# Seven products over six of eight k-tiles: a decoder layer on one core of a Trainium2 chip, with its buffers cut to make room

## The chip, the core and the metric

The kernel is one program on one core of a Trainium2 chip. The time is device microseconds (us) from start to end of one execution. Five engines run beside each other, each through its own instruction stream in order, and wait for one another by semaphores: PE (matrix products), DVE (vector), ACT (activation and copies), POOL and SP (here it only issues DMAs). PEld is PE's loading of stationary operands, which overlaps PE's products.

## What is computed

One layer with two token mixers over 2048 prompt tokens and 8 sample tokens, all in fp32:

```
xn   = rms_norm(x) * g_pre                      # 1024 columns
proj = xn @ w_in                                # 1024 x 11280, split into qkv_a z_a a_a b_a qkv_b z_b gate_a gate_b
a    = gated delta rule, 8 heads, over silu(short conv(qkv_a)), gated with silu(z_a), @ w_proj_a
b    = dilated window attention, 3 groups of 4 heads, combined by softmax weights, gated with silu(z_b), @ w_proj_b
y    = x + rms_norm((sigmoid(gate_a) * a + sigmoid(gate_b) * b) @ w_out) * g_post
```

The outputs also hold the states and caches of both mixers.

## The kernel before

**Precision.** A product in fp32 is made of three passes over operands split into a high and a low part: hi*hi, hi*lo, lo*hi. Three matmuls of one 128 x 128 block of W against one row of X stand together; the text calls them a triple (`three`, L991).

**In-projection.** The prompt is worked through in two halves of 1024 tokens, each again in two blocks of 512 (`th`). Columns of w_in come as tiles of 128, two tiles per step (`step`, L983). Of the eight k-tiles of 128 rows, the first KS = 4 go through a Winograd scheme: a 2 x 2 block product (token blocks by k halves, k halves by the two column tiles) in seven products instead of eight, each over KH = KS/2 k-tiles; the other 8 - KS are multiplied plainly (`rest`). A step is thus 7*KH + 4*(8 - KS) triples, 30 with KS = 4. In the first half a step is run twice (256 and 260 columns, the 4 extra being sample tokens), in the second once with 512 columns. There are 44 steps per half; the very first of all is a plain one (`opening`, L927). Sums of X (`sums`, L733) and of W (`wsplit`, L796) feed the seven products. X lies split and transposed in SBUF rows XS (seven sums by KH) and XP (plain k-tiles); `transpose` (L688) makes four PE transposes per row and `xevac` (L554) splits it. For the second half the rows are written anew as the last step of the first half lets go of each.

**W.** SP loads each pair of W tiles into two buffers (`raws`). `wsplit` forms sums and writes six split pieces (`evs` 0 to 5) into six slots of 512 columns; `done` in `step` gives a slot back after its last product. A step uses, in this order, products 1 (slot 0), 7 (slot 1), 6 (slot 2), 2 (slot 0), rest (3), 5 (2), 4 (slot 4), rest (3), 3 (slot 1), rest (slot 5); the last rest runs after the first product of the next step.

**The other work.** Each finished tile is copied out by `sink` (L855) into a page, one of 17 SBUF buffers of 1040 columns. `gdn` (L1212) is one delta-rule head: short conv of its k, q and v tiles (`conv`, L1174), decay tables, an inverse by 31 small steps on a lane buffer (`inverse`, L1359), and a loop over 8 chunks through the state `st`. `attn` (L1479) is one head of one group, `combine` joins three. `sample_gdn` and `sample_attn` work on the sample tokens during the second half. `final` (L1740) makes the last three products for four token groups.

**What sets the order.** A planner at build time (`Scheduler`, L87) runs all these as coroutines with costs and priorities and writes each engine's stream. A string, `ORDER` (L2171), sets in which order column tiles are projected: G is a head's k, q, v tiles, Z its gate tile, a one attention group (every fourth a is the z tile), g an output gate, x and y the claims for the second half's X, S, T, C those of the sample work and the conv state. In that same order page claims (`claim`, `admitter`) are granted, first come first served, out of as many tokens as there are pages: a claim that does not fit holds back all claims behind it, and `sink` holds its PSUM bank until its tile's claim is granted. A head claims 1 + 1 + 4 + 1 pages and 1 for its gate tile; `gdn` gives one back after its q part and one after its v part. `claim_page(keep)` in `final` takes a page only while more than `keep` are free.

Of the kernel before, what the change touches and what calls it, by code (L numbers as in the profile page):

```python
# [26 lines left out]
KS = 4  # L27
# [426 lines left out]
def build(nc, tc, ctx, I, O):  # L454
# [18 lines left out]
    NPAGE = 17  # L473
# [3 lines left out]
    wslots = Pool([(tl(f"wh{i}", [128, 512], F32R), tl(f"wl{i}", [128, 512], F32R)) for i in range(6)])  # L477
    tbuf = tl("wt", [128, 2 * KH, 128])
# [8 lines left out]
    szg = tl("szg", [128, 12, NB])  # L487
# [79 lines left out]
    def xsamples(pg):  # L567

        page = yield Acquire(pages, 1)
        fxs = page[:, :96].rearrange("p (k t c) -> p k t c", t=2, c=4)  # L570
# [27 lines left out]
    def prep(hf, b, admit):  # L598
# [11 lines left out]
        def scales():  # L610
            st["s2"] = yield Acquire(pages, 1)
            g = I["g_pre"]
            yield K.load(st["s2"][:, :w], bass.AP(tensor=g.tensor, offset=g.offset, ap=[[0, 128], [1, w]]))
# [74 lines left out]
    def transpose(hf, st, keys, summed=None):  # L688
        pg, m = st["pg"], 128 * KH
        for key in keys:  # L690
# [7 lines left out]
            else:  # L698
                n, k = key
                o = 128 * k + m * (n in (2, 3, 4))  # L700
                if n == 6:
                    src = [st["s2"][:, m * i + o:m * i + o + 128] for i in range(4)]
                else:
                    src = [pg[4 * (n in (4, 5)) + i][:, o:o + 128] for i in range(4)]
# [28 lines left out]
    def sums(st, ev):  # L733
        m = 128 * KH
        for i in range(4):
            p, q, s2 = st["pg"][i], st["pg"][4 + i], st["s2"][:, m * i:m * i + m]
# [6 lines left out]
    def transposed1(hf, st, toks):  # L743
# [10 lines left out]
        pages.release(*(pg[i] for i in range(4, 8)), st["s2"])  # L754
        tok.release(*toks, st["toks"][4])
# [3 lines left out]
        if hf == 0:  # L759
            yield Wait(xs_ev[1])  # L760
            pages.release(pg[8])
            tok.release(*st["toks"][5:])
# [25 lines left out]
    def wput(src, ev):  # L788

        hi, lo = slot = yield Acquire(wslots, 1)  # L790
        n = src.shape[1]
        yield K.copy(hi[:, :n], src)
        yield K.tt(lo[:, :n], src, hi[:, :n].bitcast(F32), OP.subtract)
        ev.set(slot)

    def wsplit():  # L796
        for at, (kind, us, evs) in enumerate(jobs):
# [4 lines left out]
            if kind == "ab":  # L802
# [3 lines left out]
                slot = yield Acquire(wslots, 1)  # L806
# [5 lines left out]
            elif kind == "plain":  # L812
                m = 128 * KH
                for j in range(2):
                    yield from wput(f[j][:, :2 * m], evs[j])
                    yield from wput(f[j][:, 2 * m:], evs[2 + j])
                T = tbuf.rearrange("p a b -> p (a b)")
                for j in range(2):
                    yield K.tt(T[:, m * j:m * j + m], f[j][:, m:2 * m], f[j][:, :m], OP.subtract)
                yield from wput(T[:, :2 * m], evs[4])  # L820
            elif kind == "pair":
# [3 lines left out]
                T = tbuf.rearrange("p a b -> p (a b)")  # L825
                t1, t2 = (T[:, m * j:m * j + m] for j in range(2))
                yield from wput(f[0][:, :2 * m], evs[0])
                yield K.tt(t1, b12, b11, OP.subtract)
                yield K.tt(b12, b22, b12, OP.subtract)
                yield from wput(f[1][:, :2 * m], evs[1])  # L830
                yield K.tt(t2, b22, t1, OP.subtract)
                yield from wput(T[:, :2 * m], evs[2])
                yield from wput(r1, evs[3])
                yield K.tt(b21, b21, t2, OP.subtract)
                yield from wput(b21, evs[4])
                yield from wput(r2, evs[5])
            else:
                if at < len(jobs) - 2:
                    for j in range(2):
                        yield from wput(f[0][:, 512 * j:512 * j + 512], evs[1 + j])  # L840
# [14 lines left out]
    def sink(t, th, gi, c0, n, bank, pool):  # L855
# [43 lines left out]
        if t.left == 0:  # L899
# [4 lines left out]
            elif k == "z" and t.half == 0:  # L904
                yield K.pcopy(szg[:, t.idx, :], pg[:, HT:HT + NB])
# [21 lines left out]
    def opening(work):  # L927
# [3 lines left out]
        for th in range(2):  # L931
# [17 lines left out]
            if th == 1:  # L949
                wslots.release(*(e.val for e in evs[:5]))  # L950
            for gi, (c0, w) in enumerate(gemm_groups(0)):
                yield from ab_tile(0, tab, evab, th, gi, c0, w, mainb[2 * gi])
        wslots.release(evab[0].val)

    def ab_tile(hf, t, evs, th, gi, c0, w, pool):
# [12 lines left out]
    def inproj(hf, work):  # L968
# [3 lines left out]
        for at, (kind, tiles, evs) in enumerate(work):  # L972
            slots = {}
            for gi, (c0, w) in enumerate(gemm_groups(hf)):
                if kind == "ab":
                    for th in range(2):
                        yield from ab_tile(hf, tiles[0], evs, th, gi, c0, w, mainb[2 * th])
                    wslots.release(evs[0].val)
# [4 lines left out]
    def step(hf, tiles, evs, slots, gi, c0, w, end, last):  # L983
# [7 lines left out]
        def three(acc, key, hl, off, first, final):  # L991
            hi, lo = (x[:, off:off + 128] for x in hl)
# [5 lines left out]
        def product(acc, n, slot, off, first=False):  # L998
            hl = yield from wk(slot)
            for k in range(KH):  # L1000
                yield from three(acc, (n, k), hl, off + 128 * k, first and k == 0, k == KH - 1)
                if last:
                    if hf == 0:
                        xfree[n, k].set()
                    else:
# [12 lines left out]
        def done(*ns):  # L1018
            if end:
                wslots.release(*(slots[n] for n in ns))  # L1020
# [66 lines left out]
    seb = tl("seb", [128, 2, GH, NB])  # L1087

    def ab_tables(hf, t, work):
# [62 lines left out]
        if hf == 0:  # L1152
# [9 lines left out]
            yield K.copy(seb.rearrange("p a h b -> p (a h b)"), bank[:, :128])  # L1162
            side.release(bank)
        pages.release(ab, pg, tmp, cmat)
# [47 lines left out]
    def gdn(hf, h, tk, tq, tv, tz, work, done):  # L1212
# [57 lines left out]
        tok.release(toks.pop())  # L1270
# [3 lines left out]
        tok.release(toks.pop())  # L1274
# [41 lines left out]
    def gdn_q(tq, kT, e, row, sm, tb, h, ev):  # L1316
        qT = yield from conv(tq)
        gp = yield Acquire(pages, 1)
        yield K.load(gp[:, :HT], bass.AP(tensor=row.tensor, offset=row.offset, ap=[[0, 128], [1, HT]]))
# [24 lines left out]
        pages.release(gp)  # L1344
# [385 lines left out]
    def wcols(slot, off, n):  # L1730

        o = off % 512
        return [x[:, o:o + n] for x in slot[off // 512]]
# [182 lines left out]
    def sample_gdn(tiles, abdone):  # L1916
# [25 lines left out]
        pg = yield Acquire(pages, 1)  # L1942
        for i in range(2):
# [409 lines left out]
```

## Time and profile before

| | |
|---|---|
| median of 3 runs (lowest to highest) | 3048.79 us (3048.49 to 3049.93) |
| profiled execution: its own time | 3050.04 us |
| profiled execution: span from first to last instruction | 3048.2 us |
| PE, PEld, DVE, ACT, POOL busy share of the span | 99%, 88%, 72%, 40%, 5% |
| mean granted share of PE's clock | 0.996 |
| instructions | 55885 |

PE's busy time counts overlapping matmuls once, so what a matmul costs is read from the distance of one start to the next. "Idle before" is how long an engine stood still ahead of an instruction, with what ended it. PEclk is the granted share of full clock.

### The profile page before, as it was taken

The page shows a single profiled execution, that of the slowest core. Times are in us where ns is not written, and L with a number is a line of the kernel's source. Part 1 is how long each engine was busy: PE and PEld are TensorE (multiplying, and loading weights), DVE is VectorE, ACT ScalarE, POOL GpSimd, SP SyncE. Part 2 cuts the span into 40 slices and gives each one's busy share as a digit, 9 for nine tenths or more (in the row PEclk, how much of TensorE's full clock was granted, in tenths as well). Part 3 has the DMA queues.
Part 4 walks back from the last instruction along what each step waited for, and adds up shares of the span by engine and source line. Part 5 has one row for each costly group of instructions (what it writes and reads, how often), then busy time and mean ns, then how long its engine had stood idle before and what let it go on. Part 6 is the DMA issues. An engine that isn't in the chain of part 4 may idle for free.

```text
span 3048.2 us, 55885 instructions
## 1 busy us (share of the span) xinstructions
PE 3010.0 (99%) x20879; PEld 2692.0 (88%) x20879; DVE 2199.2 (72%) x5978; ACT 1212.9 (40%) x3444; POOL 141.1 (5%) x239
## 2 busy tenths in 40 slices
PE   7999999999999999999999999999999999999999
PEld 7999999999999999978887888888888888897887
DVE  6777767786778686767586868597988486666765
ACT  5545444344435443433442534343434343313121
POOL 1000000000000000000000000000000000000000
PEclk9999999999999999999999999999999999999999
DMA  4323242332233325332244332336452236565463
GB/s 125 94 73 89 58 112 71 99 85 83 70 98 89 89 79 147 110 85 81 73 121 124 88 88 80 105 96 186 137 158 86 76 100 180 176 204 197 149 226 117
DMA packets 468760, 343.46 MB, mean 113 GB/s; under 512 B 88745, under 2 KB 411825, under 8 KB 468480
## 3 DMA queue, kind: packets, MB, share of 16 engines
q1 hardware_dynamic: 468488, 339.89, 38.1%
q8 instruction: 164, 2.69, 0.4%
q14 instruction: 108, 0.88, 0.1%
HBM read 261.40 MB, written 80.97 MB: 112 GB/s over the span
## 4 chain that ended last, share of the span: by engine, by line
PE 94%; DVE 3%; DMA 2%; ACT 1%; issue 0%; SPq 0%; POOL 0%; DVEq 0%; POOLq 0%; ACTq 0%
PE bank L251 89%; PE bank L267 5%; DVE pg L311 1%; DMA wr<-in_w_in 0%; DVE wl L316 0%; DVE pg L316 0%; SPq L400 0%; DMA pg<-in_cache_v_w 0%; DMA pg<-in_x_prompt 0%; DMA pg<-in_state_gdn 0%; DMA pg<-gate 0%; ACT L280 0%; DMA ghh<-in_g_head_norm 0%; DVE wh L355 0%; DVE junk L311 0%
## 5 line engine op out<-in xcount | busy, mean ns | idle before, releaser
L280 ACT ACTIVATE pg<-bank 128x256 f32<-128x256 f32 (+7 forms) x741 | 331.8, 460 | 759.4 <-PE bank L251 690.0
L316 DVE TENSOR_TENSOR wl<-wr,wh 128x512 fp32r<-128x512 f32 x595 | 383.5, 647 | 21.3 <-ACT wh L280 3.3
L355 DVE CAST wh<-wr 128x512 fp32r<-128x512 f32 (+1 forms) x384 | 153.0, 399 | 206.9 <-PE bank L251 184.0
L251 PE MATMUL bank<-xp7s,wh 128*128 128x512 f32 (+3 forms) x1196 | 302.1, 328 | 0.0
L251 PE MATMUL bank<-xp6s,wh 128*128 128x512 f32 (+3 forms) x1132 | 290.1, 330 | 0.0
L251 PE MATMUL bank<-xp5s,wh 128*128 128x256 f32 (+3 forms) x1100 | 276.3, 327 | 0.0
L280 ACT ACTIVATE wh<-wr 128x512 fp32r<-128x512 f32 (+1 forms) x213 | 129.8, 611 | 351.9 <-PE bank L251 292.1
L251 PE MATMUL bank<-xp4s,wh 128*128 128x260 f32 (+2 forms) x1068 | 267.5, 326 | 1.6 <-DVE xp4s L311 1.6
L316 DVE TENSOR_TENSOR bank<-bank,etmp 128x256 f32<-128x256 f32 (+2 forms) x260 | 134.9, 519 | 129.4 <-PE bank L251 126.3
L251 PEld LDWEIGHTS bank<-xp7s,wh 128*128 128x128 f32 x1196 | 198.4, 188 | 17.5 <-issue 1.7
L251 PEld LDWEIGHTS bank<-xp6s,wh 128*128 128x128 f32 (+1 forms) x1132 | 189.2, 188 | 17.2 <-issue 0.8
L251 PEld LDWEIGHTS bank<-xp5s,wh 128*128 128x128 f32 (+1 forms) x1100 | 183.0, 188 | 14.7 <-issue 0.2
L251 PE MATMUL bank<-xp7s,wl 128*128 128x512 f32 (+3 forms) x592 | 195.0, 329 | 0.0
L251 PEld LDWEIGHTS bank<-xp4s,wh 128*128 128x128 f32 x1068 | 176.1, 188 | 14.9 <-DVE xp4s L311 1.8
L280 ACT ACTIVATE prob<-bank 128x512 f32<-128x512 f32 (+4 forms) x224 | 105.2, 482 | 208.7 <-PE bank L251 120.8
L311 DVE SCALAR_TENSOR_TENSOR pg<-pg,convw,pg 128x1024 f32<-128x1024 f32 x144 | 183.9, 1277 | 2.8 <-ACT pg L280 1.3
L251 PE MATMUL bank<-xp6s,wl 128*128 128x512 f32 (+2 forms) x560 | 184.9, 330 | 0.0
L251 PE MATMUL bank<-xp5s,wl 128*128 128x512 f32 (+2 forms) x544 | 178.5, 328 | 0.0
L251 PE MATMUL bank<-xs1k,wh 128*128 128x512 f32 (+4 forms) x708 | 177.8, 334 | 0.0
L251 PE MATMUL bank<-xp4s,wl 128*128 128x256 f32 (+2 forms) x528 | 172.5, 327 | 0.0
L251 PE MATMUL bank<-xs6k,wh 128*128 128x512 f32 (+3 forms) x680 | 171.3, 334 | 0.0
L251 PE MATMUL bank<-xs7k,wh 128*128 128x512 f32 (+3 forms) x680 | 169.9, 333 | 0.0
(302 smaller groups left out, 7474.8 us busy)
## 6 DMA issues: line engine op xcount, KB each, us to landing
wr<-in_w_in SPq DMA_DIRECT2D x176, 512.0 KB
pg<-in_x_prompt SPq DMA_DIRECT2D x32, 512.0 KB
pg<-grow SPq DMA_DIRECT2D x32, 512.0 KB
wr<-in_w_proj_a SPq DMA_DIRECT2D x32, 512.0 KB
wr<-in_w_out SPq DMA_DIRECT2D x32, 512.0 KB
pg<-og SPq DMA_DIRECT2D x24, 520.0 KB
pg<-gate SPq DMA_DIRECT2D x24, 512.0 KB
out<-pg SPq DMA_DIRECT2D x20, 512.0 KB
```

The costliest lines, as they stand in the source:

```text
L251: nc.tensor.matmul(out, lhsT, rhs, start=start, stop=stop, skip_group_check=shared)
L267: nc.tensor.transpose(out, in_, ident[:k, :k])
L280: return ("act", c, lambda: nc.scalar.activation(out, in_, func, **kw))
L311: lambda: nc.vector.scalar_tensor_tensor(out, in0, scalar, in1, op0=op0, op1=op1, **kw))],
L316: return ("dve", self._vcost(out, in0, in1), lambda: nc.vector.tensor_tensor(out, in0, in1, op=op))
L355: alts.append(("dve", self._vcost(out, in_, fast=True), lambda: nc.vector.tensor_copy(out, in_)))
```

## The change

KS goes from 4 to 6: seven products over three k-tiles each and two plain k-tiles. More rows of X are kept (25 instead of 22), and to make room:

- 15 pages instead of 17; a head claims 3 work pages instead of 4 and gives none back early; prep claims rise (7 to 8 and 5 to 6), as the X sums now take two pages.
- The W slots become three kinds: 3 of 768 columns (pieces 0 to 2), 1 of 384 (piece 4 and the small a/b tile), 2 of 256 (pieces 3 and 5). Sums of W are made in place in the raw buffers, and the buffer `wt` goes.
- `conv` works in place in halves of 512 columns through the four `prob` buffers, which attention, inverse and others share.
- `gdn_q` puts the decay row into the one lane buffer that `inverse` also uses, instead of a page.
- Two small tables (`szg`, `seb`) move to DRAM; 12 POOL copies become 12 DMA stores, with one more store and three loads.
- `ORDER` is another string for both halves.
- At the end of the second half three freed X rows become W slots.

```diff
-KS = 4
+KS = 6
-    NPAGE = 17
+    NPAGE = 15
-    wslots = Pool([(tl(f"wh{i}", [128, 512], F32R), tl(f"wl{i}", [128, 512], F32R)) for i in range(6)])
-    tbuf = tl("wt", [128, 2 * KH, 128])
+    wslots, wthird, wrest = Pool([]), Pool([]), Pool([])
+    for i, (pool, w) in enumerate([(wslots, 256 * KH)] * 3 + [(wthird, 128 * KH)] + [(wrest, 128 * (8 - KS))] * 2):
+        pool.free.append((tl(f"wh{i}", [128, w], F32R), tl(f"wl{i}", [128, w], F32R), pool))
...
-    def wput(src, ev):
-        hi, lo = slot = yield Acquire(wslots, 1)
-        n = src.shape[1]
-        yield K.copy(hi[:, :n], src)
-        yield K.tt(lo[:, :n], src, hi[:, :n].bitcast(F32), OP.subtract)
+    def wput(parts, ev, pool=wslots):
+        hi, lo, _ = slot = yield Acquire(pool, 1)
+        c = 0
+        for src in parts:
+            v = slice(c, c := c + src.shape[1])
+            yield K.copy(hi[:, v], src)
+            yield K.tt(lo[:, v], src, hi[:, v].bitcast(F32), OP.subtract)
         ev.set(slot)
...
-                yield from wput(f[0][:, :2 * m], evs[0])
-                yield K.tt(t1, b12, b11, OP.subtract)
+                yield from wput([f[0][:, :2 * m]], evs[0])
+                yield K.tt(b11, b12, b11, OP.subtract)
                 yield K.tt(b12, b22, b12, OP.subtract)
-                yield from wput(f[1][:, :2 * m], evs[1])
-                yield K.tt(t2, b22, t1, OP.subtract)
-                yield from wput(T[:, :2 * m], evs[2])
-                yield from wput(r1, evs[3])
-                yield K.tt(b21, b21, t2, OP.subtract)
-                yield from wput(b21, evs[4])
-                yield from wput(r2, evs[5])
+                yield from wput([f[1][:, :2 * m]], evs[1])
+                yield K.tt(b22, b22, b11, OP.subtract)
+                yield from wput([b11, b22], evs[2])
+                yield from wput([r1], evs[3], wrest)
+                yield K.tt(b21, b21, b22, OP.subtract)
+                yield from wput([b21], evs[4], wthird)
+                yield from wput([r2], evs[5], wrest)
...
     def conv(t):
-        cp = yield Acquire(pages, 1)
-        c, w = cp[:, :HT], convw[:, t.idx]
-        yield K.scaled(c, pg[:, 3:3 + HT], w[:, 3:4])
-        for i in (2, 1, 0):
-            yield K.stt(c, pg[:, i:i + HT], w[:, i:i + 1], c, OP.mult, OP.add)
-        yield K.act(pg[:, :HT], c, AF.Tanh, scale=0.5)
-        yield K.stt(c, pg[:, :HT], 1.0, c, OP.add, OP.mult)
-        pages.release(pg)
-        return cp
+        for o in (0, HT // 2):
+            c = yield Acquire(prob_t, 1)
+            yield K.scaled(c, pg[:, o + 3:o + 3 + HT // 2], w[:, 3:4])
+            for i in (2, 1, 0):
+                yield K.stt(c, pg[:, o + i:o + i + HT // 2], w[:, i:i + 1], c, OP.mult, OP.add)
+            yield K.act(pg[:, o:o + HT // 2], c, AF.Tanh, scale=0.5)
+            yield K.stt(pg[:, o:o + HT // 2], pg[:, o:o + HT // 2], 1.0, c, OP.add, OP.mult)
+            prob_t.release(c)
+        return pg
...
-        tok.release(toks.pop())
         toks = toks + (yield Wait(tv.admit))
...
-        tok.release(toks.pop())
...
     def gdn_q(tq, kT, e, row, sm, tb, h, ev):
         qT = yield from conv(tq)
-        gp = yield Acquire(pages, 1)
+        ln = yield Acquire(lanes, 1)
+        gp = ln[0]
...
-    ORDER = ("GZaaGaZaGaagZGgaZagGZaagGagagZGagaZGaZagggggggxgyg",
-             "gGgZggaagGaZSagGaZaGaZgaggGaagTZGaZaCggGaaZgGZaggag")
+    ORDER = ("GaaGZgaaZGaaZGZagagGZaagGaaZggGaagZGgagZagggggxgyg",
+             "GZgaaggGagSagZgGaaZGaggZaGagagTgZGggaZagGaaGZZaggaC")
...
-            preps = [[claim(7), claim(4)], None]
+            preps = [[claim(8), claim(4)], None]
...
-            work = claim(4)
+            work = claim(3)
```

## Rows read from the trace of the kernel before

**Rows 1.** The page: busy time of each engine; the chain that ended last, by engine.
```profile
PE 3010.0 (99%) x20879; PEld 2692.0 (88%) x20879; DVE 2199.2 (72%) x5978; ACT 1212.9 (40%) x3444; POOL 141.1 (5%) x239
...
PE 94%; DVE 3%; DMA 2%; ACT 1%; issue 0%; SPq 0%; POOL 0%; DVEq 0%; POOLq 0%; ACTq 0%
```

**Rows 2.** Timeline of PE, one step of the first half (start us, duration us).
```profile
1002.83 0.40 PE L251 MATMUL bank<-xs1k,wh 128*128 128x256 f32 x2
...
1013.49 0.40 PE L251 MATMUL bank<-xs1k,wh 128*128 128x260 f32 x2
...
1024.15 0.60 PE L267 MATMUL bank<-cst,pg 128*128 128x128 f32 x4
1024.51 0.36 PE L251 MATMUL bank<-xp7s,wl 128*128 128x260 f32 x1
1024.71 0.40 PE L251 MATMUL bank<-xs1k,wh 128*128 128x256 f32 x2
```

**Rows 3.** Timeline of PE, two triples of the second half.
```profile
1929.70 0.63 PE L251 MATMUL bank<-xs1k,wh 128*128 128x512 f32 x2
...
1930.39 0.62 PE L251 MATMUL bank<-xs1k,wh 128*128 128x512 f32 x2
```

**Rows 4.** Groups of DVE by form: count, busy us, mean ns of one.
```profile
L316 DVE TENSOR_TENSOR wl<-wr,wh 128x512 fp32r<-128x512 f32 x508 | 347.0, 686 | 20.2 <-ACT wh L280 3.3 <-PE bank L251 2.3
L311 DVE SCALAR_TENSOR_TENSOR pg<-pg,convw,pg 128x1024 f32<-128x1024 f32 x144 | 183.9, 1277 | 2.8 <-ACT pg L280 1.3
L355 DVE CAST wh<-wr 128x512 fp32r<-128x512 f32 x314 | 133.0, 423 | 197.2 <-PE bank L251 175.2 <-DMA wr<-in_w_out 11.0 <-DMA wr<-in_w_in 3.8
...
L311 DVE SCALAR_TENSOR_TENSOR pg<-pg,pg 128x1024 f32<-128x1024 f32 x48 | 58.5, 1218 | 8.7 <-ACT pg L280 8.6
...
L316 DVE TENSOR_TENSOR wl<-wr,wh 128x256 fp32r<-128x256 f32 x87 | 36.5, 420 | 1.0
...
L355 DVE CAST wh<-wr 128x256 fp32r<-128x256 f32 x69 | 19.8, 287 | 9.7 <-PE bank L251 8.8
...
L316 DVE TENSOR_TENSOR pg<-pg,pg 128x512 f32<-128x512 f32 x24 | 16.5, 686 | 0.3
...
L311 DVE SCALAR_TENSOR_TENSOR pg<-pg,ssxb,pg 128x512 f32<-128x512 f32 x12 | 8.8, 746 | 2.6 <-POOL ssxb L367 2.6
```

**Rows 5.** Groups of ACT by form: the copies of W.
```profile
L280 ACT ACTIVATE wh<-wr 128x512 fp32r<-128x512 f32 x194 | 121.9, 631 | 339.5 <-PE bank L251 291.0 <-DMA wr<-in_w_out 18.7 <-DMA wr<-in_w_proj_a 12.9
...
L280 ACT ACTIVATE wh<-wr 128x256 fp32r<-128x256 f32 x18 | 7.5, 417 | 11.3 <-DVE wr L316 11.3
```

**Rows 6.** Windows: length, busy us of PE, PEld, DVE, ACT, POOL; PEclk, DMA share, GB/s.
```profile
0.00:20.00 20.00, 8.05 (x45) 7.22 (x46) 12.82 (x29) 10.08 (x19) 4.35 (x12) 1.00 0.85 287
...
2100.00:2400.00 300.00, 295.55 (x1728) 246.51 (x1726) 244.24 (x782) 120.20 (x327) 14.93 (x20) 0.98 0.46 130
```

**Rows 7.** The same view, the stretch where the second half begins.
```profile
1270.00:1280.00 10.00, 7.42 (x56) 6.61 (x54) 9.61 (x22) 5.13 (x11) 0.00 (x0) 1.00 0.32 110
1280.00:1300.00 20.00, 19.50 (x106) 17.04 (x107) 15.12 (x28) 9.21 (x16) 0.00 (x0) 0.91 0.22 58
```

**Rows 8.** Timeline of DVE: first and last chunk of the first head's loop.
```profile
239.17 0.35 DVE L311 SCALAR_TENSOR_TENSOR rr<-bank,tneG,pg 128x128 f32<-128x128 f32 x1 [2.32 <-PE bank L251]
...
265.98 0.34 DVE L311 SCALAR_TENSOR_TENSOR rr<-bank,tneG,pg 128x128 f32<-128x128 f32 x1
```

**Rows 9.** By tile: conv weights (three per tile); loop chunks, eight per head (ns min/median/max, first to last start).
```profile
L311 DVE SCALAR_TENSOR_TENSOR pg<-pg,convw,pg x144: 1232/1277/1286, 79.2 to 2500.4; 128x1024 f32<-128x1024 f32 x144
...
L311 DVE SCALAR_TENSOR_TENSOR rr<-bank,tneG,pg x128: 331/349/353, 239.2 to 2639.9; 128x128 f32<-128x128 f32 x128
```

**Rows 10.** By tile: bias loads that open each attention group; stores that close it.
```profile
L400 SPq DMA_DIRECT2D bias<-brep_d x24: 342/432/1353, 98.0 to 2476.7; - x24
...
L400 SPq DMA_DIRECT2D og<-pg x80: 360/534/2097, 156.1 to 2573.5; - x80
```

**Rows 11.** By tile: the sample work's load of its inputs; a table's last use in it.
```profile
L400 SPq DMA_DIRECT2D snew_d<-pg x24: 319/348/355, 58.7 to 1095.4; - x24
L400 SPq DMA_DIRECT2D pg<-snew_d x1: 420/420/420, 1510.4 to 1510.4; - x1
...
L311 DVE SCALAR_TENSOR_TENSOR pg<-pg,seb,bank x64: 335/340/348, 1551.9 to 1760.6; 128x128 f32<-128x128 f32 x64
```

**Rows 12.** By tile: the lane buffer's loads and the stores that end its use.
```profile
L400 SPq DMA_DIRECT2D lane_t<-in_c_consts x16: 352/423/1266, 127.9 to 2476.2; - x16
L400 SPq DMA_DIRECT2D tl<-lane_t x16: 319/344/667, 173.8 to 2527.8; - x16
```

More of the change, by code (lines that the diff above doesn't have):

```diff
@@ L486, in build @@
     snew_d = dr.tile([128, 24, NB], F32, name="snew_d")
-    szg = tl("szg", [128, 12, NB])
+    szg_d = dr.tile([128, 12, NB], F32, name="szg_d")
+    seb_d = dr.tile([128, 2 * GH * NB], F32, name="seb_d")
+    seb_ev = Event()
     ssm = tl("ssm", [128, 3, 12, NB])
@@ L701, in transpose @@
                 if n == 6:
-                    src = [st["s2"][:, m * i + o:m * i + o + 128] for i in range(4)]
+                    src = [st["s2"][i // 2][:, m * (i % 2) + o:m * (i % 2) + o + 128] for i in range(4)]
                 else:
@@ L753, in transposed1 @@
         yield from transpose(hf, st, keys, ev)
-        pages.release(*(pg[i] for i in range(4, 8)), st["s2"])
-        tok.release(*toks, st["toks"][4])
+        pages.release(*(pg[i] for i in range(4, 8)), *st["s2"])
+        tok.release(*toks, *st["toks"][4:6])
         yield Wait(st["done0"])
@@ L991, in three @@
         def three(acc, key, hl, off, first, final):
-            hi, lo = (x[:, off:off + 128] for x in hl)
+            hi, lo = (x[:, off:off + 128] for x in hl[:2])
             xh, xl = (v[:, c0:c0 + w] for v in xrow(key))
@@ L1004, in product @@
                         xfree[n, k].set()
+                    elif k == 2 and n < 4:
+                        x = XS[n][k]
+                        wslots.release((x[:, 0:512], x[:, 512:1024], wslots))
                     else:
@@ L1019, in done @@
             if end:
-                wslots.release(*(slots[n] for n in ns))
+                wfree(*(slots[n] for n in ns))
         t1, t2 = tiles
@@ L1161, in ab_tables @@
             yield K.mm(bank[:, :128], ones[:NB, :], ab[:NB, :128])
-            yield K.copy(seb.rearrange("p a h b -> p (a h b)"), bank[:, :128])
+            yield K.copy(tmp[:, :128], bank[:, :128])
             side.release(bank)
+            yield K.load(seb_d, tmp[:, :128])
+            seb_ev.set()
         pages.release(ab, pg, tmp, cmat)
@@ L1343, in gdn_q @@
         yield K.tt(qT[:, :HT], qT[:, :HT], gp[:, :HT], OP.mult)
-        pages.release(gp)
+        lanes.release(ln)
         ev.set((qT, qk))
@@ L1732, in wcols @@
         o = off % 512
-        return [x[:, o:o + n] for x in slot[off // 512]]
+        return [x[:, o:o + n] for x in slot[off // 512][:2]]
     def three(w, x, n, s0, sn):
@@ L1986, in sample_gdn @@
         for h in range(GH):
-            S.spawn(sample_head(h, vn, sg_t, pg, kq, qk_b, os_, left, all_done), 15, f"sample{h}")
+            S.spawn(sample_head(h, vn, sg_t, pg, kq, qk_b, os_, seb, left, all_done), 15, f"sample{h}")
         yield Wait(all_done)
@@ L2225, in build @@
             elif what == "x":
-                preps[1] = [claim(5)]
+                preps[1] = [claim(6)]
             elif what == "y":
```

57 lines of the change are left out of this document (32 added, 25 removed).

## The prediction, made before the changed kernel ran

> **What bounds the kernel now.** I read the page first: PE is busy for 3010 of 3048 us and holds 94% of the chain that ended last, DVE 3% [rows 1]. A busy share alone proves little, as overlapping matmuls hide how fast PE issues, so I then read starts in PE's timeline. In the first half, 30 triples of 256 columns take 1002.83 to 1013.49, 0.355 us each; the next 30, of 260, take until 1024.71 with four transposes (0.36) among them, 0.362 each [rows 2]. In the second half a triple of 512 columns takes 0.69 us, 231 ns per matmul [rows 3]. These runs have no gap in them: PE is issue-bound in the in-projection, and a matmul left out there shortens the end, unless PE then waits for something. What could make it wait is read from the windows and from how long buffers are held.
>
> **PE, removed.** A step goes from 7x2 + 4x4 = 30 triples to 7x3 + 4x2 = 29. Second half: 44 steps x 0.69 = 30.4 us. First half: 43 steps (the opening is plain) x (0.355 + 0.362) = 30.8 us. Together **-61.2 us**.
>
> [...]
>
> **PE, added.** Three more rows of X per half, four transposes each: 6 x 0.36 [rows 2] = **+2.2 us**.
>
> **The start.** Before the first product, three things grow from 512 to 768 columns. The first scaling on DVE takes 256 columns more; 1277 against 746 ns for 1024 and 512 [rows 4] is 1.04 ns per column, so +0.27 us. The g_pre row for it is 128 KB longer, 0.46 us at the 287 GB/s of the first 20 us [rows 6]. The first hi piece of W, on ACT, grows by 256 x (631 - 417)/256 = 0.21 us [rows 5]. Sum 0.94, **+1.0 us**; between nothing, if DMA and copies overlap, and 2 us.
>
> **Where the second half begins.** [...] Three more rows are three more subtractions of 0.69 [rows 4], and W's share of DVE in that step grows by 1.4 us (below): **+3.5 us**, between nothing and twice that.
>
> **DVE, per step.** Subtractions for the low parts, by piece: before, five of 512 columns and one of 256; now pieces 0 and 1 of 768, piece 2 in two of 384, piece 4 of 384, pieces 3 and 5 of 256. From 686 and 420 ns [rows 4], a column is 1.04 ns: 384 is 553, 768 is 952. Before 5 x 686 + 420 = 3850 ns, after 2 x 952 + 3 x 553 + 2 x 420 = 4403. The four sums of W: 4 x 420 become 4 x 553, +0.53 us. Casts, where DVE makes them, 5 x 423 + 287 = 2402 to about 2757 (559 at 768, 355 at 384). In all 1.4 us per step, about 120 us over 87 steps. Conv in halves: three of 746 twice instead of three of 1277, and 686 twice instead of 1218 [rows 4], +0.8 us x 48 tiles = 38 us. DVE then has some 2360 us of work in 3000, 79% against 72%; in its fullest long stretch, 2100 to 2400, where it has 244 of 300 us [rows 6], about 88%. The cover is DVE's idle time; priced at nothing there, and as a rival below.
>
> **W's slots, a new wait.** Before, piece 2 (t1, t2) went into the slot that piece 4 left, 18 triples ahead of its use in the next step's product 6. Now three wide slots serve pieces 0 to 2, and piece 2 must wait for product 3: rest (2 triples), product 1 (3), the tail (2), product 7 (3), so 10 triples, 3.6 us in the first half and 6.9 in the second. It needs a copy of 384 on ACT (524 ns) and two subtractions of 553, 1.6 us, plus the crossings between engines. Pieces 3 to 5 and the release of the raw buffers queue behind it in `wsplit`. Two microseconds are to spare, two or three DVE operations: taken at nothing, up to 0.4 us per step.
>
> **Pages, the cost that I cannot read off.** No row shows PE waiting for a page before. A head holds its pages from its conv, 79.2, through its loop, 265.98, 187 us [rows 8, 9]; heads start 158 us apart (239.2 to 2639.9 for 16, eight chunks each). Before, it held five to seven pages of its claim of seven, on average six; after, six throughout. So 6 x 187/158 = 7.1 pages either way: the smaller claim is spent by giving none back early. Attention: 58 us for the first group, 97 for the last [rows 10], some 78 us every 103, of 4.3 pages in the second half: 3.3. The sample work holds four pages for 250 us [rows 11] and three for about as long, 1.4 on average over the half's 8 x 158 us; gates, z tiles and combine about 1.5. That is 13.3 pages, 78% of 17 and 89% of 15. With claims granted in order, some tile will stand at `sink` with its bank until a head's loop ends. One such gap: a loop of 26.8 us [rows 8] less half a step, which the other banks cover (158 us per head, 5.5 steps, 28.8 each: 14.4), 12.4 us; and a stop of 2.6 us was followed by a dip to 0.91 over 20 us, 1.8 us lost [rows 7]. **+14 us** per gap. I take one; bounds none and four.
>
> [...]
>
> **Edits at nothing.** The 12 stores of szg_d are of the kind of snew_d's, 0.35 us of SP each [rows 11], on a queue with slack; POOL is 5% busy. The decay row in the lane buffer waits while `inverse` has it: 46 us (127.9 to 173.8) [rows 12], and v's conv and the next head's inverse stand behind it; but the loop needs the inverse's result anyway, which comes later still (239.2). Conv now takes one of four `prob` buffers, 4.3 us per half tile, 96 times: it lengthens attention a little, within the page term. The extra ACT time is hidden at 40% busy. The last stage uses the same number of X rows and W slots.
>
> **The sum.** From the profiled execution's own time: 3050.0 - 61.2 + 2.2 + 1.0 + 3.5 + 14 = 3009.5 us. The median of the runs stands 1.25 us below that execution: **3008 us**. A measurement of this kernel can tell about 0.2%, 6.1 us.
>
> **The rivals.**
> *Pages run out (A).* The same mechanism at many places instead of one: in the second half every head would stop its successor's tiles, worst while the sample work holds its four pages and at the end, where two gate tiles are claimed only after the last head's claim, and `final` wants four free pages before it starts. For: 89% mean occupancy, strict order, no early give-back. Against: not a single such wait now, and the new order of tiles spreads gates more evenly. After the other terms 54.5 us are left, so it decides from the fourth gap on: four gaps give 3050, six 3050.0 - 54.5 + 84 - 1.25 = 3078 us, slower. Three give 3036.
> *DVE and the slots pace the steps (B).* 87 steps x 0.4 us = 35 us, with one gap 3043, without 3029. For: 10 triples instead of 18, DVE at 88% where it is fullest. Against: in steps like that of [rows 2, 3] PE never waited for W.
> *No added waits (C).* 3008 - 14 = 2994, or 2988 if the start and the turn to the second half cost nothing either.
> *The saving does not arrive (D).* If PE's spare 12% of weight loading [rows 1] meant that another limit sets the pace, the time would stay near 3049. Against: back-to-back starts at one distance.
>
> **How the numbers follow.** Forecast (one or two gaps, 3000 to 3025) 0.50; C 0.13; A 0.24, of which 0.07 with three gaps, 0.05 with four and 0.12 beyond; B 0.10, nearly all faster; D 0.03. Faster 0.50 + 0.13 + 0.07 + 0.09 = 0.79, same 0.05 + 0.04 = 0.09, slower 0.12. The range 2990 to 3044 holds the forecast, most of C, three gaps and B, and leaves out four gaps and more, D and the best of C, about 0.2.
>
> **What would show it.** Right: 29 triples per step at 0.69 and about 0.36 us; PE's busy time some 59 us lower; idle time on PE grown by some 15 to 25 us, in few places, one of them ahead of in-projection matmuls with DVE and ACT idle too (a page), another where the second half begins; DVE near 79%. Wrong towards A: several stops over 10 us after 1500 us, or a late start of the last stage. Wrong towards B: short waits of xs6k products for wl, in most steps. Wrong towards C: PE's idle time as before.

## The result, and the profile after

The changed kernel takes **2999.98 us** (median of four runs, 2998.97 to 3005.6) against 3049.11 us of the kernel before (four runs, 3048.49 to 3049.93): a ratio of 0.9843 [0.9825, 0.986], 49 us less. The forecast of 3008 us was 8 us too high, and the range held the time. The sum behind it was right in its largest term. Its total came out as near as it did partly by luck: the term for pages was wrong, and what it left out offset the error.

The page, busy time by engine, to set beside [rows 1]:

```profile
PE 2956.3 (99%) x20513; PEld 2640.2 (88%) x20513; DVE 2349.9 (78%) x6281; ACT 1239.3 (41%) x3622; POOL 126.0 (4%) x228
```

PE has 366 matmuls fewer: 44 steps x 3 and 43 steps x 2 x 3 make 390 that go, 24 transposes come. PE is busy for 53.7 us less, DVE for 151 us more. One step of the first half on PE's timeline of the changed kernel (start us, duration us), as in [rows 2]:

```profile
1010.90 0.40 PE L251 MATMUL bank<-xs1k,wh 128*128 128x260 f32 x2
1011.14 0.28 PE L251 MATMUL bank<-xs1k,wl 128*128 128x260 f32 x1
...
1016.02 0.60 PE L267 MATMUL bank<-cst,pg 128*128 128x128 f32 x4
...
1022.15 0.40 PE L251 MATMUL bank<-xs1k,wh 128*128 128x256 f32 x2
```

Each product now has three triples of the same xs name (xs1k here). From 1010.90 to 1022.15 there are 29 triples and two groups of four transposes of 0.36: (11.25 - 0.72) / 29 = 0.363 us per triple, where [rows 2] gave 0.362. Triples are as dear as before; there is one fewer in each step. In the second half, two starts one triple apart:

```profile
1564.87 0.62 PE L251 MATMUL bank<-xs3k,wh 128*128 128x512 f32 x2
...
1565.56 0.63 PE L251 MATMUL bank<-xs3k,wh 128*128 128x512 f32 x2
```

That is 0.69 us, as in [rows 3].

Groups of DVE by form, to set beside [rows 4] (count, busy us, mean ns of one):

```profile
L311 DVE SCALAR_TENSOR_TENSOR prob<-pg,convw,prob 128x512 f32<-128x512 f32 x288 | 214.5, 746 | 4.0 <-ACT prob L280 0.3
L316 DVE TENSOR_TENSOR wl<-wr,wh 128x768 fp32r<-128x768 f32 x176 | 167.5, 952 | 4.2 <-ACT wh L280 0.9 <-DVE pg L311 0.2
L316 DVE TENSOR_TENSOR wl<-wr,wh 128x384 fp32r<-128x384 f32 x263 | 145.1, 552 | 4.3 <-ACT wh L280 0.9 <-PE bank L251 0.4
...
L311 DVE SCALAR_TENSOR_TENSOR pg<-pg,prob 128x512 f32<-128x512 f32 x96 | 66.0, 688 | 18.2 <-ACT pg L280 17.5
```

The sizes are the predicted ones (952 and 553). These two parts of the convolution take 214.5 + 66.0 us instead of 183.9 + 58.5, 38.1 us more, as worked out.

What PE waited for, in the view of waits (us in total, times, longest):

```profile
PE bank L267 <- DVE ssx L301: 9.3, 1, 9.3
PE bank L267 <- DVE pg L316: 7.3, 4, 3.2
...
PE bank L251 <- ACT ww L280: 2.1, 5, 0.4
...
PE bank L251 <- DVE wl L316: 0.9, 2, 0.7
```

and the first two of these in the kernel before:

```profile
PE bank L267 <- DVE ssx L301: 8.5, 1, 8.5
...
PE bank L267 <- DVE pg L316: 3.1, 2, 1.7
```

PE stood for W's low parts 0.9 us in the whole run. The largest wait after the start is that for the sums of X (line 316) where the second half begins: 7.3 us, 3.1 us before.

**A reading that the prediction did without.** The in-projection can stop while PE stays busy. The view that shows it is that of windows restricted to the tile `wh`: its PE column then counts only the matmuls that read W's high part. Such a row holds length, busy us of PE, PEld, DVE and ACT, then the granted clock, DMA share and GB/s. The kernel before, at 2300:

```profile
2300.00:2305.00 5.00, 1.71 (x4) 0.77 (x4) 0.68 (x1) 0.36 (x1) 1.00 0.52 122
2305.00:2310.00 5.00, 0.00 (x0) 0.00 (x0) 0.00 (x0) 0.00 (x0) 0.77 0.15 41
2310.00:2315.00 5.00, 0.00 (x0) 0.00 (x0) 0.00 (x0) 0.00 (x0) 0.55 0.74 226
2315.00:2320.00 5.00, 0.00 (x0) 0.00 (x0) 0.00 (x0) 0.00 (x0) 0.79 0.55 154
```

and the same windows with all that the engines did (POOL's column added):

```profile
2305.00:2310.00 5.00, 3.51 (x16) 2.83 (x17) 4.05 (x9) 2.97 (x11) 0.48 (x1) 0.77 0.15 41
2310.00:2315.00 5.00, 4.91 (x22) 4.04 (x22) 2.85 (x9) 0.28 (x1) 0.53 (x1) 0.55 0.74 226
2315.00:2320.00 5.00, 3.91 (x24) 3.52 (x23) 2.56 (x9) 2.40 (x14) 0.00 (x0) 0.79 0.55 154
```

For 20.5 us (2302.4 to 2322.9 between starts on PE's timeline) no in-projection product ran, and PE, 70 to 98% busy, had a head's loop and some attention alone, 10.2 us of it at half clock (a granted share of 0.50, from 2307.7 to 2314.5 and from 2317.9 to 2321.3). No single idle time of PE in it is longer than 0.74 us. I call this a **stop** below. The changed kernel has one of 10.5 us at 2453:

```profile
2450.00:2455.00 5.00, 2.36 (x6) 0.99 (x6) 0.42 (x1) 0.00 (x0) 1.00 0.46 120
2455.00:2460.00 5.00, 0.00 (x0) 0.00 (x0) 0.00 (x0) 0.00 (x0) 1.00 0.02 3
2460.00:2465.00 5.00, 1.37 (x4) 0.67 (x4) 0.00 (x0) 0.00 (x0) 1.00 0.73 199
```

It lost more where the second half begins (the text calls this the turn). The same restricted view, beside [rows 7]:

```profile
1235.00:1240.00 5.00, 3.19 (x12) 2.04 (x12) 2.51 (x5) 0.41 (x1) 1.00 0.20 80
1240.00:1245.00 5.00, 0.00 (x0) 0.00 (x0) 1.30 (x3) 0.83 (x2) 0.66 0.64 166
1245.00:1250.00 5.00, 0.00 (x0) 0.00 (x0) 0.00 (x0) 0.00 (x0) 0.50 0.24 72
1250.00:1260.00 10.00, 4.30 (x10) 1.97 (x10) 0.00 (x0) 0.00 (x0) 0.91 0.01 2
```

The turn is a stop of 12.5 us (7.4 before), and the granted clock is 0.50 for all of 1245 to 1250. In all it is at half for 10.2 us around this stop, and PE has work in only 5.8 of them; before it was 3.4 us, with work in 3.2.

### The profile page after: what moved, and what is told of

Read it like the earlier page. It is cut to its first block, busy times and chain, and to the rows that moved or that the text cites. A ratio compares the mean times of both kernels' runs of the same rounds, so it can differ in the third digit from the quotient of the medians.

```text
span 2998.5 us, 55647 instructions
## 1 busy us (share of the span) xinstructions
PE 2956.3 (99%) x20513; PEld 2640.2 (88%) x20513; DVE 2349.9 (78%) x6281; ACT 1239.3 (41%) x3622; POOL 126.0 (4%) x228
## 4 chain that ended last, share of the span: by engine, by line
PE 93%; DVE 3%; issue 2%; DMA 1%; ACT 0%; SPq 0%; POOL 0%; DVEq 0%; POOLq 0%; ACTq 0%
PE bank L251 88%; PE bank L267 5%; DVE wl L316 1%; DMA wr<-in_w_in 0%; DVE wr L316 0%; DVE pg L311 0%; DMA pg<-ya_d 0%; DVE junk L311 0%; DVE wh L355 0%; DVE pg L316 0%; DMA pg<-og 0%; SPq L400 0%; DVE prob L311 0%; DMA out<-pg 0%; DMA pg<-in_state_gdn 0%
## 5 line engine op out<-in xcount | busy, mean ns | idle before, releaser
L280 ACT ACTIVATE pg<-bank 128x256 f32<-128x256 f32 (+6 forms) x737 | 332.6, 464 | 634.3 <-PE bank L251 575.3
L316 DVE TENSOR_TENSOR wl<-wr,wh 128x384 fp32r<-128x384 f32 (+3 forms) x693 | 433.5, 635 | 17.3 <-ACT wh L280 6.5
L251 PE MATMUL bank<-xp7s,wh 128*128 128x256 f32 (+4 forms) x1116 | 283.9, 329 | 0.0
L251 PE MATMUL bank<-xp6s,wh 128*128 128x256 f32 (+3 forms) x1092 | 278.6, 329 | 0.0
L251 PE MATMUL bank<-xs1k,wh 128*128 128x512 f32 (+5 forms) x894 | 223.3, 334 | 0.0
L311 DVE SCALAR_TENSOR_TENSOR prob<-pg,convw,prob 128x512 f32<-128x512 f32 x288 | 214.5, 746 | 4.0 <-ACT prob L280 0.3
L251 PE MATMUL bank<-xs2k,wh 128*128 128x256 f32 (+5 forms) x878 | 214.6, 327 | 0.0
L251 PE MATMUL bank<-xs5k,wh 128*128 128x260 f32 (+4 forms) x846 | 202.3, 325 | 0.0
L251 PE MATMUL bank<-xs4k,wh 128*128 128x256 f32 (+4 forms) x822 | 194.8, 324 | 0.0
L251 PE MATMUL bank<-xs3k,wh 128*128 128x256 f32 (+2 forms) x792 | 193.8, 328 | 0.0
L316 DVE TENSOR_TENSOR bank<-bank,etmp 128x256 f32<-128x256 f32 (+2 forms) x260 | 134.7, 518 | 58.5 <-PE bank L251 52.6
```

Of the source, the lines that this page charges most:

```text
L251: nc.tensor.matmul(out, lhsT, rhs, start=start, stop=stop, skip_group_check=shared)
L280: return ("act", c, lambda: nc.scalar.activation(out, in_, func, **kw))
L311: lambda: nc.vector.scalar_tensor_tensor(out, in0, scalar, in1, op0=op0, op1=op1, **kw))],
L316: return ("dve", self._vcost(out, in0, in1), lambda: nc.vector.tensor_tensor(out, in0, in1, op=op))
```

## The experiments

Twelve kernels ran, each beside the kernel before. "Clock loss" is (1 - mean granted clock) x span of the profiled run; it counts time at half clock whether PE had work in it or not. "Stops" are all stretches over 10 us between starts of in-projection products on PE's timeline, ahead of the last stage, the turn to the second half in a column of its own. "k-tiles" is over how many of the eight the seven products run (four before, six after). The kernel before took 3049 to 3052 us (medians) beside the different runs, so a difference between two of these rows is good to some 3 us.

| kernel | k-tiles, pages, order | median us | clock loss | turn | stops, us |
|---|---|---|---|---|---|
| before | 4, 17, old | 3049.1 | 12 | 7.4 | 20.5 |
| e6 | 4, 17, new | 3037.3 | 9 | 7.9 | none |
| e9 (room) | 4, 17, new | 3032.3 | 9 | 7.5 | none |
| e12 (room, conv in quarters) | 4, 17, new | 3036.6 | 9 | 7.7 | none |
| e1 (room) | 4, 15, new | 3061.6 | 28 | 7.7 | 17.4 |
| e2 | 4, 15, old | 3107.3 | 50 | 11.3 | four, 99 in all |
| **after** | 6, 15, new | **3000.0** | 21 | 12.5 | 10.5 |
| e5 (conv in quarters) | 6, 15, new | 3039.6 | 39 | 17.8 | 26.6, 11.1, 38.6 |
| e3 | 6, 15, old | 3133.5 | 88 | 17.2 | eight, 156 in all |
| e10 | 6, 14, new | 3125.5 | 88 | 19.6 | nine, 204 in all |
| e4 (sums on POOL) | 6, 15, new | 3001.0 | 27 | 15.0 | 10.5 |
| e7 (sums early) | 6, 15, new | 2994.6 | 24 | 9.0 | 11.4 |
| **e8** (and X earlier) | 6, 15, new | **2992.7** | 15 | 8.3 | 10.5 |
| e11 (and gates moved) | 6, 15, new | 3012.4 | 33 | 8.3 | 31.9 |

### The parts of the change, taken apart

**e1: the room without the products.** The changed kernel with the seven products back on four k-tiles and W's slots of one width:

```diff
-KS = 6
+KS = 4
-    wslots, wthird, wrest = Pool([]), Pool([]), Pool([])
-    for i, (pool, w) in enumerate([(wslots, 256 * KH)] * 3 + [(wthird, 128 * KH)] + [(wrest, 128 * (8 - KS))] * 2):
+    wslots = wthird = wrest = Pool([])
+    for i, (pool, w) in enumerate([(wslots, 512)] * 6):
```

> The changed kernel with KS back at 4 and everything else of the change kept (15 pages, small claims, conv in halves, lane row, tables in memory, new order); W in six slots of 512 from one pool. Theory 1 (PE's issue sets the time, making room is nearly free): 30 triples per step again, +59 us on PE less the relief at the start and at the turn to the second half (about 5 us): 3050 to 3057 us, DVE about 120 us less busy. Rival (making room costs something that the seven products pay for): 3060 us or more. Rival (order and room are a gain of their own, and the products brought less than 59 us): 3045 us or less.

Measured: 3061.58 us (3059.39 to 3064.14), ratio to before 1.0037 [1.0023, 1.005]. The rival was right. Making room costs 12 us net, and the products then bring 3061.6 - 3000.0 = 61.6 us. The windows restricted to `wh` show a stop, 17.4 us from 943.1, that the changed kernel does not have:

```profile
945.00:950.00 5.00, 0.00 (x0) 0.00 (x0) 0.00 (x0) 0.00 (x0) 0.81 0.00 2
950.00:955.00 5.00, 0.00 (x0) 0.00 (x0) 0.00 (x0) 0.00 (x0) 0.50 0.00 0
955.00:960.00 5.00, 0.00 (x0) 0.00 (x0) 0.00 (x0) 0.00 (x0) 0.50 0.01 3
```

**e6: the new order alone**, on the kernel before:

```diff
-    ORDER = ("GZaaGaZaGaagZGgaZagGZaagGagagZGagaZGaZagggggggxgyg",
-             "gGgZggaagGaZSagGaZaGaZgaggGaagTZGaZaCggGaaZgGZaggag")
+    ORDER = ("GaaGZgaaZGaaZGZagagGZaagGaaZggGaagZGgagZagggggxgyg",
+             "GZgaaggGagSagZgGaaZGaggZaGagagTgZGggaZagGaaGZZaggaC")
```

> The kernel before, with its 17 pages and its old claims, with the new order of the tiles alone. Theory 1 (the new order is there for the smaller pool and does nothing where pages are plenty): 3044 to 3056 us. Rival 1 (it is the order itself that costs the some 11 us of making room, as it puts the sample work beside other products): 3057 us or more, half clock 50 us or more. Rival 2 (the order is better anyway): under 3043 us.

Measured: 3037.27 us (3036.45 to 3037.92), ratio 0.9961 [0.9947, 0.9975]: rival 2. The order saves 12 us by itself, and the stop of 20.5 us is gone.

**e9: the room with 17 pages**, that is e1 with two pages given back:

```diff
-    NPAGE = 15
+    NPAGE = 17
```

> The run that made the room without the two further products (3061.6 us), with 17 pages again instead of 15; the convolution stays in place by halves, the claims small, the tables in memory, the order new. The kernel before with the new order alone took 3037.3 us, so that all of this costs 24 us. Theory 1 (the two pages are what costs: a tile without a page stops the in-projection, and PE is left with a head's loop alone): 3034 to 3043 us, no stretch of over 10 us without an in-projection product except in the last stage. Rival (the convolution by halves and the other work on DVE cost it, as the heads take longer): 3055 us or more.

Measured: 3032.32 us (3031.36 to 3043.75), ratio 0.9942 [0.992, 0.9964]. Theory 1 holds, the time 1.7 us below its range: the convolution in place, the small claims and the tables in memory cost nothing (5 us less than e6, though the slowest of e9's four runs lies above all of e6's). The two pages cost 3061.6 - 3032.3 = **29 us**. The clock loss grew by 28 - 9 = 19 us beside it, and not all of that lies in the stop: of e1's time at half clock, 17.1 us stand there, and 10.2 at 1812 and 6.8 at 2573 stand where the in-projection does not stop.

So the 49 us are made up as: new order -12, other edits for room -5, two pages fewer +29, two more k-tiles in the products -62. By the ratios, each to the kernel before beside it, they are -12, -6, +29 and -59.

### Pages

**e2: the kernel before with 15 pages** (`NPAGE = 17` to `15`), and **e3: the changed kernel with the old order** (e6's diff turned round).

> The kernel before with 15 pages instead of 17, nothing else. Theory 1 (mean occupancy of 13.4 pages: 15 pages with the old claims and order bind): several gaps of 10 us and more on PE, most of them in the second half: 3080 us or more. Rival (two of the 17 pages were spare): 3049 us, within 4 us, and no gap on PE over 3 us after the start.

> The changed kernel with the old order of column tiles; claims, pages and products stay. Theory 1 (the new order is what makes 15 pages do): gaps on PE of 10 us and more, 3015 us or more. Rival (the smaller claims make 15 pages do, the order does nothing): 3000 us, within 6 us.

Measured: e2 3107.3 us (3096.01 to 3109.25), ratio 1.0178 [1.0152, 1.0204]; e3 3133.48 us (3127.57 to 3138.27), ratio 1.0273 [1.0254, 1.0291]. Theory 1 in both by the time, not by its gaps on PE: they are stops, and the longest single idle time of PE in them is 5.8 us in e2 and 5.9 in e3. With the old order 15 pages cost 58 us on the kernel before, twice the 29 us of e9 to e1; those two have the new order and the smaller claims, so this pair does not tell order from claims. e3 does: everything else is the changed kernel's, and it loses 133 us. The order is not an extra; without it the smaller claims do not make 15 pages do.

**e10: the changed kernel with 14 pages** (`NPAGE = 15` to `14`).

> The changed kernel with 14 pages instead of 15. Theory 1 (the pages bind, and with each page fewer there are more stretches in which PE has a head's loop alone): 3025 to 3060 us, two or more stretches of over 10 us without an in-projection product. Rival (the smaller claims left room, so that one page fewer is hardly noticed): 2998 to 3010 us.

Measured: 3125.54 us (3122.17 to 3129.95), ratio 1.024 [1.0222, 1.0258]: 125 us for one page, twice the worst that was expected. The first of its nine stops, 19.0 us at 36, is at the start, with PE on transposes of X. Windows restricted to `wh`, another one, of 37.5 us:

```profile
928.00:938.00 10.00, 0.00 (x0) 0.00 (x0) 0.00 (x0) 0.00 (x0) 0.78 0.00 1
938.00:948.00 10.00, 0.00 (x0) 0.00 (x0) 0.00 (x0) 0.00 (x0) 0.88 0.16 33
948.00:958.00 10.00, 0.00 (x0) 0.00 (x0) 0.00 (x0) 0.00 (x0) 0.63 0.16 47
```

Its page, and in its view of waits the trace of a loop that runs by itself, PE standing briefly for each link of the chain:

```profile
PE 3036.3 (97%) x20513; PEld 2692.5 (86%) x20513; DVE 2357.0 (75%) x6260; ACT 1244.1 (40%) x3647; POOL 125.2 (4%) x224
```

```profile
PE bank L267 <- DVE pg L316: 19.8, 7, 11.2
PE bank L251 <- ACT ww L280: 14.0, 35, 0.7
```

(2.1 us in 5 waits for `ww` in the changed kernel.) These short waits are the visible part of a stop: PE's idle time, span less busy, grew by 50 us (3128.1 - 3036.3 against 2998.5 - 2956.3), and the run lost 125. The rest is busy time: the same 20513 matmuls took PE 80 us more, beside 88 - 21 = 67 us more clock loss.

### DVE

**e5: the convolution in quarters** on the changed kernel, and **e12: the same on e9**, with 17 pages:

```diff
-        for o in (0, HT // 2):
-            c = yield Acquire(prob_t, 1)
+        for o in range(0, HT, HT // 4):
+            cb_ = yield Acquire(prob_t, 1)
+            c = cb_[:, :HT // 4]
...
```

> The changed kernel with the convolution of each tile cut into quarters instead of halves: the same sums on 256 columns, twice as many instructions. Per tile six DVE instructions of 746 ns and two of 686 become twelve of about 480 and four of about 420, some 1.6 us more for each of 48 tiles, about 80 us of DVE work in all. Theory 1 (DVE has room, so that what the change added there was rightly priced at nothing): 2994 to 3007 us, PE's waits for wl as few as now (0.9 us). Rival (DVE, now 78% busy, begins to pace the steps): PE waits for wl or for the evacuation of banks, 3020 us or more.

> The run with the room but 17 pages and without the further products (3032.3 us), with the convolution in quarters, which cost 39.6 us on the changed kernel with its 15 pages. It adds the same some 75 us of DVE work. Theory 1 (DVE itself has room; its work costs time only because tiles and heads then hold their pages longer and 15 do not suffice): 3028 to 3042 us, no stretch of over 10 us without in-projection products ahead of the last stage. Rival (DVE's work lies on the path whatever the pages): 3055 us or more.

Measured: e5 3039.57 us (3034.97 to 3045.91), ratio 0.9968 [0.9958, 0.9978]; e12 3036.59 us (3033.4 to 3037.08), ratio 0.9952 [0.9935, 0.9969]. The page's busy times, e5, then e12, then e9, the run that e12 is to be set beside:

```profile
PE 2974.8 (98%) x20513; PEld 2650.8 (87%) x20513; DVE 2420.7 (80%) x6730; ACT 1252.6 (41%) x3749; POOL 128.1 (4%) x228
```

```profile
PE 3003.5 (99%) x20879; PEld 2688.9 (89%) x20879; DVE 2332.0 (77%) x6751; ACT 1263.4 (42%) x3717; POOL 128.4 (4%) x221
```

```profile
PE 3001.1 (99%) x20879; PEld 2686.6 (89%) x20879; DVE 2265.8 (75%) x6310; ACT 1242.8 (41%) x3582; POOL 126.0 (4%) x221
```

In both DVE gets some 70 us more work (2349.9 to 2420.7; 2265.8 to 2332.0). With 17 pages that costs 4 us, less than e9's own runs spread, with 15 pages 40 us. In e5 theory 1 of its own expectation fell, but the form that its rival gave was not what came: PE does not wait for W's low parts, it has three stops. The longest, in the view restricted to `wh`:

```profile
2470.00:2480.00 10.00, 0.00 (x0) 0.00 (x0) 0.00 (x0) 0.00 (x0) 0.67 0.00 0
2480.00:2490.00 10.00, 0.00 (x0) 0.00 (x0) 0.00 (x0) 0.00 (x0) 0.61 0.23 70
```

Some 5 of the 40 us are DVE's directly: at the turn PE waited for the sums of X for 12.1 us, 7.3 in the changed kernel. DVE's work was hidden from PE where pages were to spare, and was paid where they were not. That it does so by letting tiles and heads keep their pages longer is argued, not shown. What the traces hold of it is small: from a head's first conv instruction on DVE to the last chunk of its loop (tiles `convw` and `rr`, mean of 16 heads) it is about 183 us in e5 against 180 in the changed kernel, and about 183 in e12 against 179 in e9, some 2% longer in both. How long attention and the gates held theirs was not measured. The two pairs also differ in how many k-tiles the products take, so pages are not the only difference between them.

### The turn to the second half

**e4: two of the three differences of X on POOL.**

```diff
-            yield K.tt(a11, a22, s2, OP.subtract)
-            yield K.tt(a12, a12, s2, OP.subtract)
+            yield K.ptt(a11, a22, s2, OP.subtract)
+            yield K.ptt(a12, a12, s2, OP.subtract)
```

> The changed kernel with two of the three subtractions per tile in the sums of X (8 of 12 per half, 0.55 us each on DVE) given to POOL. Theory 1 (the turn to the second half waits for DVE's sums): PE's waits for them, 7.3 us, shrink by 2 to 5 us and the low clock behind them by 3 to 7 us: 2992 to 2997 us. Rival (POOL takes longer for the same and the transposes wait for POOL instead): 3000 us or more, with the same gap at 1240 us put down to POOL.

Measured: 3001.02 us (2996.86 to 3006.65), ratio 0.9841 [0.9822, 0.9859], no gain: the rival. POOL needs 1115 ns for one, twice as long as DVE does in the changed kernel (552 ns), and the subtractions left on DVE took 850 ns each beside it. PE waited 9.8 us for POOL, and the turn became longer, 15.0 us. The changed kernel's line, then two of e4:

```profile
L316 DVE TENSOR_TENSOR pg<-pg,pg 128x384 f32<-128x384 f32 x24 | 12.3, 552 | 0.3
```

```profile
L316 DVE TENSOR_TENSOR pg<-pg,pg 128x384 f32<-128x384 f32 x8 | 6.6, 850 | 0.0
...
L367 POOL TENSOR_TENSOR pg<-pg,pg 128x384 f32<-128x384 f32 x16 | 17.4, 1115 | 29.1 <-DVE pg L316 29.1
```

**e7: the sums early, on DVE.** The four sums and four of the twelve differences overwrite nothing that is still to be transposed:

```diff
-        yield Wait(st["first"])
+        if hf == 0:
+            yield Wait(st["first"])
...
             yield K.tt(pg[4 + i][:, :m], pg[4 + i][:, :m], pg[4 + i][:, m:2 * m], OP.add)
+            if hf == 1:
+                s2 = st["s2"][i // 2][:, m * (i % 2):m * (i % 2) + m]
+                yield K.tt(s2, pg[4 + i][:, :m], pg[i][:, :m], OP.subtract)
+        if hf == 1:
+            yield Wait(st["first"])
```

> The changed kernel; for the second half the four sums and the first four of the twelve differences of X, which overwrite nothing that is still to be transposed, are issued as soon as X is scaled, not after the first transposes. That takes 8 x 0.55 = 4.4 us of DVE work out of the stretch in which PE waits 7.3 us. Theory 1 (these sums are what the turn waits for): the wait falls to 2 to 4 us and the half clock after it from 10.2 us to 3.4 or less, 2990 to 2996 us. Rival (DVE is full ahead of the turn too, so W's pieces come later instead): 2997 to 3004 us, waits for wl at the turn.

**e8: and X claimed two gate tiles sooner** (the first half's order ends in `gggxggygg` instead of `gggggxgyg`).

> As the run with the early sums, and the second half's X (eight pages and four) claimed two gate tiles sooner, so that DVE has its work earlier, where it has more room. Theory 1 (DVE's share of the turn is what counts): 2986 to 2994 us, the wait at the turn under 3 us. Rival (twelve pages held longer stop the last gate tiles of the first half): 3000 us or more, with a gap of some us before 1240.

Measured: e7 2994.56 us (2990.42 to 3001.75), ratio 0.9824 [0.9809, 0.9838]; e8 2992.66 us (2989.68 to 2993.02), ratio 0.9813 [0.9799, 0.9826]. Both times lie in the ranges of theory 1, and the wait for the sums falls from 7.3 to 4.1 and 3.6 us, less far than it said (2 to 4, and under 3). The time at half clock after it falls from 10.2 to 6.8 us in both, where 3.4 or less was expected; the windows of all engines at 1240:1250, e7 and then e8 (the changed kernel has PE 3.89 and a clock of 0.58 there):

```profile
1240.00:1250.00 10.00, 8.13 (x44) 7.34 (x44) 8.14 (x16) 5.27 (x10) 0.00 (x0) 0.66 0.28 66
```

```profile
1240.00:1250.00 10.00, 6.40 (x29) 5.50 (x29) 8.74 (x18) 4.00 (x8) 0.00 (x0) 0.68 0.44 119
```

e8 is faster than both kernels of the case: all of its runs lie below all runs of the changed kernel. e7's gain of 5 us is the size of the turn's growth (12.5 us against 7.4), but its slowest run lies above the fastest three of the changed kernel; between e7 and e8 the runs overlap too, and their 2 us are not settled.

**e11: the last two gate tiles ahead of the last head**, on e8, against the stop that is left at 2444:

```diff
-             "GZgaaggGagSagZgGaaZGaggZaGagagTgZGggaZagGaaGZZaggaC")
+             "GZgaaggGagSagZgGaaZGaggZaGagagTgZGggaZagGaaggGZZaaC")
```

> As the run with X claimed two gate tiles sooner (2992.7 us), and in the second half the last two gate tiles stand ahead of the last head in the order, not behind it. In that run the in-projection stops for 10.5 us at 2444, with the last heads' claims granted first. Theory 1 (the tiles at that place lack a page that the last head's claim holds): the stop goes, 2980 to 2989 us. Rival (the last head then starts two tiles later and its loop ends later, which the last stage waits for, or another tile stops in their place): 2992 us or more.

Measured: 3012.44 us (3008.15 to 3017.07), ratio 0.9866 [0.9845, 0.9887]. The rival: the stop of 10.5 us went, and one of 31.9 us came at 2491. Two gate tiles moved in the order are worth 20 us.

## Why the prediction was right, and where it was not

- **PE, removed (-61.2) and added (+2.2).** Right. The triple is unchanged (0.363 and 0.69), the count of matmuls is the predicted one, and e1 to the changed kernel is -61.6 us. That figure also holds 7 us less clock loss (28 to 21) and 5.7 us more idle time of PE, so its closeness to -59 is in part luck. Rival D is out.
- **The start (+1.0).** PE's first wait grew from 8.5 to 9.3 us; the size is right and no run tells it from nothing.
- **The turn (+3.5, at most 7).** Right in kind and within its bounds, the term somewhat small: the turn's stop grew by 12.5 - 7.4 = **5.1 us**. That PE waits for DVE there is in both views of waits, 3.1 us before and 7.3 after, so by 4.2 us more; time at half clock grew by 6.8 us, but PE had work in only 2.6 of them, which by the measure of clock loss costs half of that (triples of 512 columns in the kernel before started 1.28 us apart at a granted clock of 0.50, 1625.74 to 1628.30, against 0.69 at 1.00). What PE waited for there, the sums of X, I had not priced: 16 in each half grew from 256 to 384 columns, about 2.1 us by the 420 and 553 ns of the working.
- **DVE at nothing.** Its total came as worked out (78%). But "the cover is DVE's idle time" left out a condition: e5 and e12 show about the same work at 40 us and at 4. DVE's idle time alone did not hide it; with pages to spare it was hidden.
- **W's slots, taken at nothing.** Right: 0.9 us of waits for `wl`. Rival B, 0.4 us in each of 87 steps, is refuted.
- **Pages (+14, one gap).** The step that failed is "No row shows PE waiting for a page before". It looked for idle time of PE, and a stop has little: the kernel before had one of 20.5 us (that it lacked a page there is not shown; the new order alone removes it, e6). So the base of the count was wrong, and so was the size: two pages cost 29 us (e9, e1), not 14. The new order, which I had only named as an argument against rival A, brought 12 (e6) and the other edits 5. 29 - 12 - 5 = 12 us stands against my 14, so the total came out nearly right by luck, by errors that offset each other. The sign that went with the term failed too: idle time on PE was to grow by 15 to 25 us and grew from 38.2 to 42.2 us, which I had listed as a sign of rival C. Stops, and the low clock in them, lie mostly in PE's busy time. The count of 13.3 pages, 78% of 17 and 89% of 15, pointed the right way: with 14 (95%) rival A comes true at 3125 us, with 15 and the old order at 3133. (In rival C, 2994 - 1.0 - 3.5 makes 2990, not 2988.)
- **Where a stop shows.** In the stream of in-projection products one fewer page made nine stops (e10), 204 us in all. PE's own idle time shows only a part of it (50 of 125 us), and of the stop of 20.5 us before it shows 3.4.

Open: which claim holds up which tile in the stop at 2453; why e1 stops at 943 and the changed kernel, with the same order and pages, does not; why the clock fell in e1 at 1812 and 2573; and how much of the 29 us 16 pages would give back.

## What to carry to other kernels

Where one engine is shared by a main stream and fillers, look for gaps in the main stream (windows restricted to its operand), not in the engine: a busy engine can be starved of the work that counts (PE was 70 to 98% busy in the stop of 20.5 us). Price a smaller buffer pool by a run with the old kernel and the smaller pool, or the new one with one buffer more or fewer; near the edge one buffer cost 125 us, and two gate tiles moved in the order 20, where the edit itself brought 62. Test the slack of a second engine with the buffers that the new kernel will have: the same work cost 4 us with 17 and 40 with 15.

## What was not expected of the hardware

The granted clock fell in a stretch in which PE was busy all the time; its last idle time, 1.08 us ahead of 1560.83, was 12 us back. Windows of all engines of the changed kernel:

```profile
1560.00:1570.00 10.00, 9.17 (x46) 7.69 (x46) 7.65 (x20) 2.14 (x5) 0.46 (x1) 1.00 0.00 1
1570.00:1580.00 10.00, 10.00 (x105) 7.85 (x105) 4.06 (x13) 2.71 (x7) 0.00 (x0) 0.66 0.19 54
1580.00:1590.00 10.00, 10.00 (x50) 6.71 (x50) 3.03 (x11) 2.22 (x5) 0.18 (x1) 0.65 0.44 128
1590.00:1600.00 10.00, 10.00 (x57) 8.76 (x57) 2.69 (x7) 1.15 (x3) 0.00 (x0) 0.84 0.32 84
```

What PE did just before, on its timeline:

```profile
1569.25 1.17 PE L251 MATMUL bank<-pg,pg 128*128 128x2 f32 x10
1570.35 0.69 PE L251 MATMUL bank<-prob,pg 32*32 32x32 f32 x16
1570.97 0.83 PE L251 MATMUL bank<-pg,pg 128*128 128x2 f32 x6
```

Products of two columns (the sample heads) and of 32x32 (the inverse) ran among those of 512, with no idle time on PE after 1561, and for 17.1 us between 1573 and 1593 the granted clock was 0.50 (1572.7 to 1579.6 and 1583.0 to 1593.2), some 8.5 us of clock loss. In e6, where the two kinds lay further apart (two columns at 1614 and 1640, 32x32 from 1627 to 1632), it did not fall there; at the corresponding place it did for 10.2 us in e1, 6.8 in e9 and 3.4 in the kernel before. Whether either of them brings it down was not tried. The rows show a fall after either: in e1 at 1812 after 32x32 and 64x64 ones (1804 to 1812, the last of two columns at 1801), with PE busy all the time, and in the kernel before at 1625 after 16 of two columns alone (from 1622.6, with 0.68 us of idle time ahead of them). POOL's 1115 ns for 384 columns, where DVE takes 552, was the other surprise, with DVE's own 850 beside it.
